# A bidirectional DeltaNet and mLSTM block: another pace for the triangular solve, its inverse stored by quarters, the scan placed later

## The chip, the cores and the metric

The kernel runs on one core of one Trainium2 chip. Its engines are PE (TensorE: matrix products into PSUM), DVE (VectorE), ACT (ScalarE), POOL (GpSimd) and SP (SyncE, which here only issues DMAs). Each runs its own list of instructions in order and waits for the others by semaphores. The metric is device time in microseconds; the kernel before takes 1715.46 us, the median of three runs (1714.88 to 1715.53).

## The reference

One layer on a sequence of 512 tokens of width 2048, all in float32. A normed input is projected to 13,376 columns, which feed two branches: a gated DeltaNet of 8 heads and an mLSTM of 8 heads, each run forward and backward over the sequence; a sigmoid gate mixes them. The change touches the DeltaNet branch:

```python
def gated_delta_chunked(q, k, v, g, beta):          # per direction; chunks of 64 tokens
    gc = jnp.cumsum(g, axis=-1)
    decay = jnp.exp(jnp.where(causal, gc[..., :, None] - gc[..., None, :], -jnp.inf))
    kb = k * beta[..., None]                          # k is l2-normalised over its 128 entries
    lower = jnp.where(strict, jnp.einsum("bhnik,bhnjk->bhnij", kb, k) * decay, 0.0)
    a_mat = lower + jnp.eye(CHUNK, dtype=q.dtype)
    sol = lax.linalg.triangular_solve(a_mat, rhs, left_side=True, lower=True, unit_diagonal=True)
    ...
    def step(state, inp):                             # sequential over the chunks
        v_new = u_c - jnp.einsum("bhlk,bhkv->bhlv", w_c, state)
        state_next = state * jnp.exp(gl_c)[..., None, None] + jnp.einsum("bhlk,bhlv->bhkv", kd_c, v_new)
```

## The kernel before, in words

*The stream.* The weights of all projections are cut into groups of 8 x 128 rows by 128 columns (512 KB). For each group SP loads `wr`, ACT rounds it to `wh`, DVE subtracts to get `wl` (lines 175 and 176), and PE does 24 matmuls of 128 x 512 (line 212). Groups 0 to 47 are the DeltaNet's keys, queries and values (`gk`, `gq`, `gv`), 48 to 63 its output gate `gz`, 64 to 119 the merge gates `mg0` to `mg27`, two groups each, and from 120 on come the mLSTM's inputs. Group n's tiles are called `wr`n, `wh`n and `wl`n. Four `wr` and three pairs of `wh` and `wl` are held.

*The mix.* Everything else is written as one generator, `master()`, and advanced by one `yield` (a tick) after every four matmuls of the stream (`TICK`). So a count of yields is a place in the stream, and the scheduler below that order keeps each engine's list close to it, but moves instructions back where it reckons that their data come later.

*The DeltaNet's part of the mix.* `gdn_pre(h)` forms, per head, the products `pgm`, the sums of squares `pn` and the transposes `px`, and stores what the scan needs in DRAM (`d_head`, `d_lane`). `gdn_solve` then solves all 8 heads x 2 directions x 8 chunks at once: 128 unit triangular matrices of 64 x 64, one per partition of `lx`, in 62 steps of two DVE instructions, `tm` and `lx` (lines 592 and 595). Before the first step the key norm factors are needed: `rk2` from the sums `ssk`, `brk` from it, four transposes to `pb` on PE (line 557), a store to `d_brk` and a load `bsc`. A second form of the factors, `rk` to the power -1/2 on POOL (line 606), gives `cvv` and `csp`, which the scan uses. While the steps run, ACT copies finished columns of `lx` into `l0` and `lt`, which hold the transposed inverse, 16 at a time (`copy_cols`). At the end `lx` and `l0` go to `d_sol`, and `l0` and `lt` to `d_inv` (lines 612 to 622). `gdn_load_b` reads them back per head as `xt` and `xi`.

*The scan.* Heads run in pairs. Each begins with `pw`, 16 small matmuls of `xi` (line 664), then `wx`, a second `pw`, and four chunk pairs of `vps`, `sps`, `kps` and `og`, ending with the transposes `po` (line 745). Three ticks lie between two pieces. After the scan the memory passes to the mLSTM's heads.

Of the kernel before, what the change touches and what calls it, by code (L numbers as in the profile page):

```python
# [9 lines left out]
F32 = mybir.dt.float32  # L10
F32R = mybir.dt.float32r
AF = mybir.ActivationFunctionType
ALU = mybir.AluOpType

P = 128
T = 512
NT = 4
# [3 lines left out]
EPS = 1e-6  # L21
# [8 lines left out]
LOAD_AHEAD = 4  # L30
SPLIT_AHEAD = 2
TICK = 4
SOLVE_RATE = 0.65
N_EARLY = 28


# [4 lines left out]
def hybrid_block(  # L41
# [20 lines left out]
    nc = tc.nc  # L62
# [10 lines left out]
    def pool(name, bufs=1, side="left", space=None):  # L73
        kw = {"space": space} if space is not None else {"side": side}
        if space is None or space == PSUM:
            kw["reuse_waits"] = "tile"
        return tc.tile_pool(name=name, bufs=bufs, **kw)
# [3 lines left out]
    pp = ctx.enter_context(pool("pp", bufs=2, space=PSUM))  # L81
# [4 lines left out]
    d_inv = dram.tile([2, H, 8, 64, 64], F32, name="d_inv")  # L86
# [47 lines left out]
    ones = const.tile([P, 1], F32, name="ones")  # L134
# [99 lines left out]
    egc = const.tile([P, NT, 16], F32, name="egc")  # L234
# [7 lines left out]
    ssk = const.tile([P, NT, H], F32, name="ssk")  # L242
# [215 lines left out]
    def gdn_pre(h):  # L458
        p1 = st["p1"][1]
        if h + 1 < H:  # L460
            dec_load(h + 1)
            qg_load(h + 1)

        dec = st["dec", h]
        dec4 = dec.rearrange("p d (t i) -> p d t i", i=P)
        g4 = gct.rearrange("p t (d h) -> p d t h", d=2)[:, :, :, h:h + 1]
        nc.vector.tensor_tensor(dec4, dec4, g4.broadcast_to([P, 2, NT, P]), op=ALU.subtract)
        for d in range(2):
            nc.gpsimd.affine_select(out=dec4[:, d], in_=dec4[:, d], pattern=[[0, NT], [1 - 2 * d, P]],
                                    compare_op=ALU.is_ge, fill=-1e30, base=0, channel_multiplier=2 * d - 1)  # L470
        for _ in range(3):
            yield
        nc.scalar.activation(dec, dec, AF.Exp)
        while f"gq{h}" not in done:
            yield
        ckq, qg = st["ckq", h], st["qg", h]
        sqt = p1.tile([P, T], F32, tag="sqt", name=f"sqt{h}")
        sqk = p1.tile([P, P], F32, tag="sqk", name=f"sqk{h}")
        for _ in range(4):
            yield  # L480
        nc.scalar.activation(sqt, ckq[:, 1, :], AF.Square)
        for d in range(2):
            nc.gpsimd.tensor_tensor(qg[:, d, :], qg[:, d, :], ckq[:, 1, :], op=ALU.mult)
        while f"gv{h}" not in done:
            yield
        cv = st["cv", h]
        for _ in range(4):
            yield

        pgm = [pp.tile([P, 2, 2, P], F32, tag="mix", name=f"pgm{h}{tt}") for tt in range(2)]  # L490
        for t in range(NT):
            cs = slice(t * P, (t + 1) * P)
            nc.tensor.matmul(pgm[t // 2][:, t % 2], ckq[:, 0, cs], ckq[:, :, cs], start=True, stop=True)
        pn = pp.tile([P, 8], F32, tag="st0", name=f"pn{h}", bufs=1)
        for t in range(NT):
            nc.tensor.matmul(pn[:, t:t + 1], sqt[:, t * P:(t + 1) * P], ones, start=True, stop=True)
        px = [pp.tile([P, NT, P], F32, tag="acc", name=f"px{i}{h}") for i in range(2)]
        for i, src in enumerate((ckq[:, 0, :], cv)):
            for t in range(NT):
                nc.tensor.transpose(px[i][:, t, :], src[:, t * P:(t + 1) * P], ident)  # L500
        la = p1.tile([P, 2, NT, 2, P], F32, tag="la", name=f"la{h}", bufs=2)
        kd = p1.tile([P, 2, NT, P], F32, tag="kd", name=f"kd{h}", bufs=2)
        vt = p1.tile([P, T], F32, tag="vt", name=f"vt{h}", bufs=2)
        nc.scalar.copy(vt, px[1].rearrange("p a b -> p (a b)"))
        for tt in range(2):
            for d in range(2):
                nc.vector.tensor_tensor(la[:, d, tt * 2:tt * 2 + 2], pgm[tt],
                                        dec4[:, d, tt * 2:tt * 2 + 2].unsqueeze(2).broadcast_to([P, 2, 2, P]),
                                        op=ALU.mult)
            yield  # L510
        for t in range(NT):
            nc.scalar.activation(sqk, px[0][:, t, :], AF.Square, accum_out=ssk[:, t, h:h + 1])
        nc.vector.tensor_copy(ssq[:, h, :], pn[:, 0:4])
        for d in range(2):
            nc.vector.tensor_tensor(
                kd[:, d], px[0], ekd[:, :, d * H + h:d * H + h + 1].broadcast_to([P, NT, P]), op=ALU.mult)
        yield
        dh = d_head[h]
        for a in range(2):
            hs_, os_ = half(a), half(1 - a)  # L520
            for d in range(2):
                nc.sync.dma_start(d_lane[d, h, a::2].rearrange("t j i -> j t i"), la[hs_, d, :, 0, hs_])
            nc.sync.dma_start(dh[hs_, HC_Y:HW].rearrange("p (t i) -> p t i", i=64), la[hs_, a, :, 0, os_])
        yield
        nc.sync.dma_start(dh[:, HC_AT:HC_KT].rearrange("p (d t i) -> p d t i", d=2, i=P), la[:, :, :, 1, :])
        nc.sync.dma_start(dh[:, HC_KT:HC_QG], ckq[:, 0, :])
        yield
        nc.sync.dma_start(dh[:, HC_QG:HC_Y], qg.rearrange("p a n -> p (a n)"))
        nc.sync.dma_start(dh[:, HC_V:HC_KD], vt)
        nc.sync.dma_start(dh[:, HC_KD:HC_AT], kd.rearrange("p d t i -> p (d t i)"))  # L530


    cvv = const.tile([P, NT, 2, H], F32, name="cvv")
    csp = const.tile([P, NT, 2, H], F32, name="csp")
    brh = const.tile([P, NT, H], F32, name="brh")

    def gdn_solve():
# [3 lines left out]
        rk = ln.tile([P, NT, H], F32, name="rk")  # L541
        rk2 = ln.tile([P, NT, H], F32, name="rk2")
        brk = ln.tile([P, NT, 2, H], F32, name="brk")
        l0 = ln.tile([P, 64, 64], F32, name="l0")
        lt = ln.tile([P, 64, 64], F32, name="lt")
        nc.sync.dma_start(l0, d_lane.rearrange("d h c j i -> (d h c) j i"))
        nc.vector.tensor_scalar(rk, ssk, EPS, None, op0=ALU.add)
        nc.vector.reciprocal(rk2, rk)
        beta4 = beta.rearrange("p t (d h) -> p t d h", d=2)
        bc = lambda v: v.unsqueeze(2).broadcast_to([P, NT, 2, H])  # L550
        nc.vector.tensor_scalar(rk2, rk2, -1.0, None, op0=ALU.mult)
# [22 lines left out]
        yield  # L574


        rev = l0[64:128, ::-1, ::-1]
        tr0 = l0[0:64].rearrange("p m j -> p j m")
        tr1 = lt[64:128].rearrange("p m j -> p j m")[:, ::-1, ::-1]
# [2 lines left out]
        def copy_cols(n, q):  # L582
            to, of = copies[n]
            cs = slice(q * 16, q * 16 + 16)
            nc.scalar.copy(to[:, :, cs], of[:, :, cs])

        cost = 0.0
        for c in range(1, 63):
            n = 63 - c
            tm = ln.tile([P, 1024], F32, tag="tm", name=f"tm{c}", bufs=1)  # L590
            tv = tm[:, 0:c * n].rearrange("p (j i) -> p j i", i=n)
            nc.vector.tensor_tensor(  # L592
                tv, lx[:, 0:c, c:c + 1].broadcast_to([P, c, n]),
                lx[:, c:c + 1, c + 1:64].broadcast_to([P, c, n]), op=ALU.mult)
            nc.vector.tensor_tensor(lx[:, 0:c, c + 1:64], lx[:, 0:c, c + 1:64], tv, op=ALU.add)  # L595
            cost += 0.13 + 0.0021 * c * n
            while cost > 0:
                yield
                cost -= SOLVE_RATE
            if 20 <= c < 60 and c % 5 == 0:  # L600
                next(st["la", 0])
            if c > 16 and c % 16 in (1, 3, 5):
                copy_cols(c % 16 // 2, c // 16 - 1)
            if c == 30:

                nc.gpsimd.tensor_tensor(rk, rk, mhalf.rearrange("p (t h) -> p t h", h=H), op=ALU.pow)
            if c == 60:
                nc.vector.tensor_tensor(cvv, beta4, bc(rk), op=ALU.mult)
                nc.vector.tensor_scalar(rk, rk, -1.0, None, op0=ALU.mult)
                nc.vector.tensor_tensor(csp, egc.rearrange("p t (d h) -> p t d h", d=2), bc(rk), op=ALU.mult)  # L610
        lanes = lambda v: v.rearrange("h c j i -> (h c) j i")
        nc.sync.dma_start(lanes(d_sol[0]), lx[0:64])
        nc.vector.tensor_copy(rev[:, :, 48:64], lx[64:128, :, 48:64])
        yield
        copy_cols(0, 3)
        nc.scalar.dma_start(lanes(d_inv[0]), l0[0:64])
        yield
        yield
        nc.sync.dma_start(lanes(d_sol[1]), l0[64:128])
        yield  # L620
        copy_cols(2, 3)
        nc.scalar.dma_start(lanes(d_inv[1]), lt[64:128])
        for _ in range(10):
            yield
        close_pool("ln")
# [301 lines left out]
    def master():  # L927
        yield from setup()
        for h in range(H):
            yield from gdn_pre(h)  # L930
# [3 lines left out]
        gdn_load_b(0)  # L934
        gdn_load_b(1)
        st["la"] = itertools.chain(gdn_load_a(2), gdn_load_a(3))
        for _ in range(6):
            yield
        yield from rolling([together([gdn_head(h), gdn_head(h + 1)]) for h in range(0, H, 2)], 13, 3)
        close_pool("p2")  # L940
# [358 lines left out]
```

## Time and profile before

| | |
|---|---|
| median of three runs | 1715.46 us |
| profiled execution | 1713.81 us |
| its span, first to last instruction | 1712.1 us |
| PE busy | 1670.8 us (98%) |
| DVE busy | 866.6 us (51%) |
| ACT busy | 618.5 us (36%) |
| POOL busy | 82.4 us (5%) |
| mean granted TensorE clock | 0.994 |

The share of an engine is an average over stages, so it is read by stretch. The page's row of PE in 40 slices has full slices but for the first, slice 13 (514 to 556 us) and the last; in slice 13 the row of the granted clock has its only value below 9. The chain that ended last goes through PE for 89% of the span, DVE for 6% and DMAs for 2%.

### The profile page before, as it was taken

The page shows a single profiled execution, that of the slowest core. Times are in us where ns is not written, and L with a number is a line of the kernel's source. Part 1 is how long each engine was busy: PE and PEld are TensorE (multiplying, and loading weights), DVE is VectorE, ACT ScalarE, POOL GpSimd, SP SyncE. Part 2 cuts the span into 40 slices and gives each one's busy share as a digit, 9 for nine tenths or more (in the row PEclk, how much of TensorE's full clock was granted, in tenths as well). Part 3 has the DMA queues.
Part 4 walks back from the last instruction along what each step waited for, and adds up shares of the span by engine and source line. Part 5 has one row for each costly group of instructions (what it writes and reads, how often), then busy time and mean ns, then how long its engine had stood idle before and what let it go on. Part 6 is the DMA issues. An engine that isn't in the chain of part 4 may idle for free.

```text
span 1712.1 us, 20938 instructions
## 1 busy us (share of the span) xinstructions
PE 1670.8 (98%) x8250; PEld 1403.1 (82%) x8250; DVE 866.6 (51%) x1266; ACT 618.5 (36%) x917; POOL 82.4 (5%) x117
## 2 busy tenths in 40 slices
PE   6999999999996999999999999999999999999998
PEld 6788888878884888888888888888888888888886
DVE  6865556569992433332345445454544444443342
ACT  6654444323432222343343344244333422222231
POOL 1100110010000000010000000000000000000000
PEclk9999999999998999999999999999999999999999
DMA  7577776594447875354443344344334644454222
GB/s 189 151 214 195 178 182 180 147 300 126 113 116 180 273 216 168 103 154 125 108 111 106 104 111 111 99 111 116 82 98 132 203 146 148 148 175 169 98 99 99
DMA packets 333724, 251.93 MB, mean 147 GB/s; under 512 B 38872, under 2 KB 294233, under 8 KB 332473
## 3 DMA queue, kind: packets, MB, share of 16 engines
q1 hardware_dynamic: 327952, 238.39, 48.8%
q10 hardware_dynamic: 5673, 12.19, 2.2%
q8 instruction: 65, 1.06, 0.3%
q14 instruction: 34, 0.28, 0.0%
HBM read 207.32 MB, written 43.16 MB: 146 GB/s over the span
## 4 chain that ended last, share of the span: by engine, by line
PE 89%; DVE 6%; issue 2%; DMA 2%; ACT 1%; POOL 0%; POOLq 0%; DVEq 0%; ACTq 0%; SPq 0%
PE pj_m L212 25%; PE pj_mg L212 15%; PE pj_br L212 10%; PE wo L1052 10%; PE pj_gq L212 5%; PE pj_gv L212 5%; PE pj_gk L212 4%; PE pj_gz L212 3%; DVE lx L595 2%; DVE tm L592 2%; PE og L683 1%; DVE wl L176 1%; DMA d_inv<-lt 1%; PE vps L706 1%; PE ph L885 1%
## 5 line engine op out<-in xcount | busy, mean ns | idle before, releaser
L176 DVE TENSOR_TENSOR wl<-wr,wh 128x1024 fp32r<-128x1024 f32 x270 | 332.1, 1231 | 474.7 <-ACT wh L175 132.7
L175 ACT CAST wh<-wr 128x1024 fp32r<-128x1024 f32 x270 | 284.0, 1052 | 710.4 <-PE pj_m L212 209.2
L212 PE MATMUL pj_m<-nth,wh 128*128 128x512 f32 x640 | 250.7, 392 | 0.0
L212 PE MATMUL pj_m<-ntl,wh 128*128 128x512 f32 x640 | 249.5, 390 | 0.0
L212 PE MATMUL pj_mg<-nth,wh 128*128 128x512 f32 x512 | 202.0, 395 | 0.0
L212 PE MATMUL pj_mg<-ntl,wh 128*128 128x512 f32 x512 | 200.6, 392 | 0.0
L212 PE MATMUL pj_m<-nth,wl 128*128 128x512 f32 x640 | 160.3, 391 | 0.0
L212 PEld LDWEIGHTS pj_m<-nth,wh 128*128 128x128 f32 x640 | 120.2, 188 | 24.6
L212 PEld LDWEIGHTS pj_m<-ntl,wh 128*128 128x128 f32 x640 | 120.3, 188 | 24.2
L212 PEld LDWEIGHTS pj_m<-nth,wl 128*128 128x128 f32 x640 | 119.6, 188 | 24.6
L212 PE MATMUL pj_mg<-nth,wl 128*128 128x512 f32 x512 | 130.7, 398 | 0.0
L212 PEld LDWEIGHTS pj_mg<-nth,wh 128*128 128x128 f32 x512 | 96.4, 188 | 19.6
L212 PEld LDWEIGHTS pj_mg<-ntl,wh 128*128 128x128 f32 x512 | 96.4, 188 | 19.2
L212 PEld LDWEIGHTS pj_mg<-nth,wl 128*128 128x128 f32 x512 | 95.8, 190 | 19.3
L1052 PE MATMUL wo<-wh,mh 128*128 128x512 f32 x256 | 100.1, 391 | 0.0
L1052 PE MATMUL wo<-wh,ml 128*128 128x512 f32 x256 | 99.8, 390 | 0.0
L212 PE MATMUL pj_br<-yl,wh 128*128 128x512 f32 x256 | 99.7, 390 | 0.0
L212 PE MATMUL pj_br<-yh,wh 128*128 128x512 f32 x256 | 99.7, 389 | 0.0
L1052 PE MATMUL wo<-wl,mh 128*128 128x512 f32 x256 | 72.9, 390 | 0.0
L1017 DVE TENSOR_TENSOR mgr<-pj_br,mgr 128x512 f32<-128x512 f32 x32 | 22.1, 692 | 86.5 <-PE pj_br L212 86.5
L212 PE MATMUL pj_br<-yh,wl 128*128 128x512 f32 x256 | 63.2, 389 | 0.0
L1052 PEld LDWEIGHTS wo<-wl,mh 128*128 128x128 f32 x256 | 48.1, 188 | 10.5 <-DVE wl L176 0.2
(320 smaller groups left out, 2515.2 us busy)
## 6 DMA issues: line engine op xcount, KB each, us to landing
wr<-in_w_in_dram SPq DMA_DIRECT2D x206, 512.0 KB, 4.0
wr<-in_w_out_dram SPq DMA_DIRECT2D x32, 512.0 KB, 4.1
hr<-d_head SPq DMA_DIRECT2D x16, 768.0 KB, 7.7
d_gate<-gt ACTq DMA_DIRECT2D x32, 256.0 KB, 4.2
e<-d_row SPq DMA_DIRECT2D x8, 1024.0 KB
mgr<-d_gate SPq DMA_DIRECT2D x32, 256.0 KB, 3.5
wr<-in_w_branch_gdn_dram SPq DMA_DIRECT2D x16, 512.0 KB, 4.8
wr<-in_w_branch_mlstm_dram SPq DMA_DIRECT2D x16, 512.0 KB
```

The lines of the kernel that those rows point to most:

```text
L175: nc.scalar.copy(hi[:, 0:m], self.raw[:, 0:m])
L176: nc.vector.tensor_tensor(lo[:, 0:m], self.raw[:, 0:m], hi[:, 0:m].bitcast(F32), op=ALU.subtract)
L212: nc.tensor.matmul(ps[0:m, :], l, r, start=(first and n == 0), stop=(last and n == len(jobs) - 1))
L592: nc.vector.tensor_tensor(tv, lx[:, 0:c, c:c + 1].broadcast_to([P, c, n]), lx[:, c:c + 1, c + 1:64].broadcast_to([P, c, n]), op=ALU.mult)
L595: nc.vector.tensor_tensor(lx[:, 0:c, c + 1:64], lx[:, 0:c, c + 1:64], tv, op=ALU.add)
L683: nc.tensor.matmul(po[:, t], l, r, start=not opened, stop=last)
L706: nc.tensor.matmul(vps[:, d], xt[:, d, t], rhs[d], start=True, stop=True)
L885: nc.tensor.matmul(ph[:, j - q0, :], e4[:, d, 0, t, :], vv[:, t, :], start=(n == 0), stop=True)
L1017: nc.vector.tensor_tensor(g_, ps, g_, op=ALU.mult)
L1052: nc.tensor.matmul(ps, l[:, kt, ts_], r, start=(kt == 0 and l is mh and r is hv), stop=(kt == NK - 1 and r is lv))
```

## The change

The solve's steps are spread by a lower rate, which is what one tick takes off a step's reckoned cost. `pn` is written behind the `px` transposes. `rk2` gets its own addition, and `rk`, its power, `cvv` and `csp` are placed at steps 30 and 50 of the solve, behind that step's `tm`. Each quarter of the inverse is stored right behind its copy, on ACT's queue, and the two stores of the whole are gone. The scan begins 18 ticks after the solve in place of 6.

```diff
-SOLVE_RATE = 0.65
+SOLVE_RATE = 0.56
...
-        pn = pp.tile([P, 8], F32, tag="st0", name=f"pn{h}", bufs=1)
-        for t in range(NT):
-            nc.tensor.matmul(pn[:, t:t + 1], sqt[:, t * P:(t + 1) * P], ones, start=True, stop=True)
         px = [pp.tile([P, NT, P], F32, tag="acc", name=f"px{i}{h}") for i in range(2)]
         for i, src in enumerate((ckq[:, 0, :], cv)):
             for t in range(NT):
                 nc.tensor.transpose(px[i][:, t, :], src[:, t * P:(t + 1) * P], ident)
+        pn = pp.tile([P, 8], F32, tag="st0", name=f"pn{h}", bufs=1)
+        ...
-        nc.vector.tensor_scalar(rk, ssk, EPS, None, op0=ALU.add)
-        nc.vector.reciprocal(rk2, rk)
+        nc.vector.tensor_scalar(rk2, ssk, EPS, None, op0=ALU.add)
+        nc.vector.reciprocal(rk2, rk2)
...
             nc.scalar.copy(to[:, :, cs], of[:, :, cs])
+            if n != 1:
+                src, r0 = (l0[0:64], q * 16) if n == 0 else (lt[64:128], 48 - q * 16)
+                nc.scalar.dma_start(lanes(d_inv[n // 2])[:, r0:r0 + 16], src[:, r0:r0 + 16])
...
             if c == 30:
+                with tc.issue_after(step.ins if hasattr(step, "ins") else step):
+                    nc.vector.tensor_scalar(rk, ssk, EPS, None, op0=ALU.add)
                 nc.gpsimd.tensor_tensor(rk, rk, mhalf.rearrange("p (t h) -> p t h", h=H), op=ALU.pow)
-            if c == 60:
-                ...
+            if c == 50:
+                with tc.issue_after(step.ins if hasattr(step, "ins") else step):
+                    nc.vector.tensor_tensor(cvv, beta4, bc(rk), op=ALU.mult)
+                    nc.vector.tensor_scalar(rk, rk, -1.0, None, op0=ALU.mult)
+                    nc.vector.tensor_tensor(csp, egc.rearrange("p t (d h) -> p t d h", d=2), bc(rk), op=ALU.mult)
...
         copy_cols(0, 3)
-        nc.scalar.dma_start(lanes(d_inv[0]), l0[0:64])
...
         copy_cols(2, 3)
-        nc.scalar.dma_start(lanes(d_inv[1]), lt[64:128])
...
-        for _ in range(6):
+        for _ in range(18):
             yield
```

What stands in DVE's list between the gates `ga0` and the split `wl53`, ahead of the solve, before and then in the change:

```order
L547 TENSOR_SCALAR rk_2850<-ssk_138 128x32
L548 RECIPROCAL rk2_2851<-rk_2850 128x32
L551 TENSOR_SCALAR rk2_2851<-rk2_2851 128x32
L608 TENSOR_TENSOR cvv_140<-tgs_129,rk_2850 128x64
L552 TENSOR_TENSOR brk_2852<-tgs_129,rk2_2851 128x64
L609 TENSOR_SCALAR rk_2850<-rk_2850 128x32
L572 COPY brh_142<-brk_2852 64x32
L573 COPY brh_142<-brk_2852 64x32
```

```order
L547 TENSOR_SCALAR rk2_2851<-ssk_138 128x32
L548 RECIPROCAL rk2_2851<-rk2_2851 128x32
L551 TENSOR_SCALAR rk2_2851<-rk2_2851 128x32
L552 TENSOR_TENSOR brk_2852<-tgs_129,rk2_2851 128x64
L572 COPY brh_142<-brk_2852 64x32
L573 COPY brh_142<-brk_2852 64x32
```

`cvv`, which takes POOL's result, no longer stands ahead of `brk`; it and `rk`'s sign are placed at step 50.

ACT's list at the end of the solve, from the last copy into `l0`, before and then in the change:

```order
L585 COPY l0_2853<-lx_2909 64x64x16
L585 COPY lt_2854<-lx_2909 64x64x16
L616 DMA d_inv_68<-l0_2853 64x4096
L622 DMA d_inv_68<-lt_2854 64x4096
L983 ACTIVATE gt7_4167<-pj_mg7_4013,vec_118 128x512
L175 CAST wh83_4217<-wr83_4062 128x1024
L984 DMA d_gate_76<-gt7_4167 128x512
L983 ACTIVATE gt8_4278<-pj_mg8_4176,vec_118 128x512
```

```order
L586 COPY l0_2853<-lx_2909 64x64x16
L987 ACTIVATE gt7_4072<-pj_mg7_3988,vec_118 128x512
L589 DMA d_inv_68<-l0_2853 64x1024
L988 DMA d_gate_76<-gt7_4072 128x512
L586 COPY lt_2854<-lx_2909 64x64x16
L175 CAST wh83_4111<-wr83_4026 128x1024
L589 DMA d_inv_68<-lt_2854 64x1024
L175 CAST wh84_4168<-wr84_4075 128x1024
L987 ACTIVATE gt8_4163<-pj_mg8_4081,vec_118 128x512
L988 DMA d_gate_76<-gt8_4163 128x512
```

The two stores of 64 x 4096 are stores of 64 x 1024, and the store of the gate `gt7` stands between them.

PE's list where the scan's first `pw` stands, before and then in the change:

```order
L664 MATMUL pw0_4084<-xi0_4025,hr0_3194 64x64
L212 MATMUL pj_mg9_4287<-ntl_128,wh82_4172 128x512
L212 MATMUL pj_mg9_4287<-nth_127,wl82_4173 128x512 x8
L212 MATMUL pj_mg9_4287<-nth_127,wh83_4217 128x512
L664 MATMUL pw0_4084<-xi0_4025,hr0_3194 64x64 x7
```

```order
L212 MATMUL pj_mg10_4236<-nth_127,wl84_4169 128x512 x8
L668 MATMUL pw0_4273<-xi0_4146,hr0_3230 64x64 x8
L668 MATMUL pw1_4296<-xi1_4156,hr1_3713 64x64 x8
L212 MATMUL pj_mg10_4236<-nth_127,wh85_4199 128x512
```

Between the two places lie nine more matmuls of group 82 and the 48 of groups 83 and 84; `pw` of head 1 now follows at once. On SP the load of `wr87` now stands ahead of the first `xt`, and that of `wr88` behind the last `xi` of head 1; before, both stood behind all of `hr2` and `hr3`.

## Rows read from the trace of the kernel before

**Rows 1.** Waits of PE, whole run: engine, line, releaser, total us, times, longest.

```profile
PE pw L664 <- DMA xi<-d_inv: 16.2, 1, 16.2
...
PE pb L557 <- DVE rk L609: 2.6, 1, 2.6
...
PE pn L496 <- ACT sqt L481: 1.2, 1, 1.2
```

**Rows 2.** Stretches: busy us of each engine, granted clock, DMA share, GB/s.

```profile
348.00:351.00 3.00, 0.40 (x4) 0.27 (x4) 0.74 (x5) 0.00 (x0) 2.18 (x1) 1.00 1.14 454
402.00:516.00 114.00, 114.00 (x505) 94.45 (x504) 108.17 (x114) 41.96 (x38) 0.00 (x0) 1.00 0.44 120
543.00:544.00 1.00, 1.00 (x4) 0.50 (x2) 0.01 (x1) 0.00 (x0) 0.00 (x0) 0.50 0.52 118
544.00:545.00 1.00, 1.00 (x16) 0.69 (x16) 1.00 (x1) 0.00 (x0) 0.00 (x0) 0.84 0.35 80
540.00:740.00 200.00, 200.00 (x1359) 173.80 (x1359) 77.51 (x159) 56.56 (x130) 9.73 (x14) 0.99 0.59 177
```

**Rows 3.** Timeline of PE: start, us, engine, line, operation, count, idle before.

```profile
517.78 1.98 PE L212 MATMUL pj_mg<-nth,wl 128*128 128x512 f32 x8
...
522.76 0.39 PE L212 MATMUL pj_mg<-nth,wh 128*128 128x512 f32 x1
539.31 0.44 PE L664 MATMUL pw<-xi,hr 64*64 64x64 f32 x2 [16.16 <-DMA xi<-d_inv]
```

**Rows 4.** Timeline of ACT at the solve's end (ACTq: its DMA issues).

```profile
512.50 2.07 ACT L585 COPY l<-lx 64x1024 f32<-64x1024 f32 x1 [4.35 <-DVE lx L595]
...
514.60 0.51 ACTq L616 DMA_DIRECT2D d_inv<-l  x1
516.66 1.06 ACTq L622 DMA_DIRECT2D d_inv<-lt  x1
```

**Rows 5.** Waits of SP, the DMA queue, 500 to 560 us.

```profile
SPq L643 <- DMA d_sol<-l: 8.8, 1, 8.8
...
SPq L644 <- DMA d_inv<-lt: 3.8, 1, 3.8
...
SPq L643 <- DMA d_inv<-l: 3.3, 1, 3.3
```

**Rows 6.** Timeline of SP's DMA issues.

```profile
514.47 1.89 SPq L166 DMA_DIRECT2D wr<-in_w_in_dram  x1
...
535.71 0.57 SPq L644 DMA_DIRECT2D xi<-d_inv  x1
...
538.25 0.57 SPq L644 DMA_DIRECT2D xi<-d_inv  x1
...
542.16 0.61 SPq L644 DMA_DIRECT2D xi<-d_inv  x1
```

**Rows 7.** The tile xi: its loads, from issue to landing.

```profile
DMA to landing us min/median/max: 2.4/2.4/2.4
```

**Rows 8.** DMA queues, 514 to 522, then 522 to 526: packets, MB, share.

```profile
q1 hardware_dynamic: 115, 1.62, 94.1%
...
q10 hardware_dynamic: 45, 0.74, 71.2%
```

**Rows 9.** Timeline of DVE before the solve.

```profile
344.31 0.35 DVE L548 RECIPROCAL rk<-rk 128x32 f32<-128x32 f32 x1
...
350.22 0.23 DVE L608 TENSOR_TENSOR cvv<-tgs,rk 128x64 f32<-128x64 f32 x1 [5.34 <-POOL rk L606]
350.36 0.22 DVE L552 TENSOR_TENSOR brk<-tgs,rk 128x64 f32<-128x64 f32 x1
```

**Rows 10.** Timeline of ACT, head 0.

```profile
80.49 0.61 ACT L481 ACTIVATE sqt<-ckq 128x512 f32<-128x512 f32 x1
```

**Rows 11.** Chain that ended last, the scan's end and the mLSTM's first projection.

```profile
751.53 0.87 PE po L745 x8
...
822.23 34.46 PE pj_m L212 x152
```

More of the change, by code (lines that the diff above doesn't have):

```diff
@@ L500, in gdn_pre @@
                 nc.tensor.transpose(px[i][:, t, :], src[:, t * P:(t + 1) * P], ident)
+        pn = pp.tile([P, 8], F32, tag="st0", name=f"pn{h}", bufs=1)
+        for t in range(NT):
+            nc.tensor.matmul(pn[:, t:t + 1], sqt[:, t * P:(t + 1) * P], ones, start=True, stop=True)
         la = p1.tile([P, 2, NT, 2, P], F32, tag="la", name=f"la{h}", bufs=2)
@@ L574, in gdn_solve @@
         yield
+        lanes = lambda v: v.rearrange("h c j i -> (h c) j i")
         rev = l0[64:128, ::-1, ::-1]
@@ L591, in gdn_solve @@
             tv = tm[:, 0:c * n].rearrange("p (j i) -> p j i", i=n)
-            nc.vector.tensor_tensor(
+            step = nc.vector.tensor_tensor(
                 tv, lx[:, 0:c, c:c + 1].broadcast_to([P, c, n]),
@@ L604, in gdn_solve @@
             if c == 30:
+                with tc.issue_after(step.ins if hasattr(step, "ins") else step):
+                    nc.vector.tensor_scalar(rk, ssk, EPS, None, op0=ALU.add)
                 nc.gpsimd.tensor_tensor(rk, rk, mhalf.rearrange("p (t h) -> p t h", h=H), op=ALU.pow)
-            if c == 60:
[L608 to L611, printed above, removed]
+            if c == 50:
[3 more added lines that the diff above has]
+                    nc.vector.tensor_tensor(csp, egc.rearrange("p t (d h) -> p t d h", d=2), bc(rk), op=ALU.mult)
         nc.sync.dma_start(lanes(d_sol[0]), lx[0:64])
```

## The prediction

> **What bounds the kernel now.** I read the busy line of the page first: PE works 1670.8 of 1712.1 us, so only the 41.3 us in which it stands still, and any time at a lowered clock, can be given back. The list of who waited for whom, for PE alone, came next [rows 1]: one wait of 16.2 us at the first `pw` matmul (line 664), which opens the scan and waits for `xi`, the inverse read back from `d_inv`; 2.6 us at `pb` (line 557) for the key norm factors; 1.2 us at the `pn` sums (line 496). The rest lies in the start and at the end, which the change leaves alone. Third, the table by stretches [rows 2]: between 402 and 516 us DVE works 108.17 of 114 us, so the solve runs there without a gap and its end cannot be pulled forward by another order. From 540 to 740 us, the scan, PE has no idle time at all.
>
> The stall costs more than its length. PE's timeline shows it between 522.99 and 539.31 us [rows 3], and the granted clock is 0.50 in 543 to 544 and 0.84 in 544 to 545 [rows 2]: 0.84 of the second at the two levels 0.5 and 1.0 puts the return to the 2.4 GHz level at 544.3. So from 539.3 to 544.3 PE worked at the 1.2 GHz level, and 5.0 us of work hold 2.5 us of loss. Round the shorter stall at `pb` the clock stayed at 1.00 [rows 2].
>
> Who sets the 539.31? The solve ends at 512.50, where ACT, released by DVE's `lx`, starts the last copies; the two 1 MB writes of `d_inv` leave ACT's queue at 514.60 and 516.66 [rows 4]. SP, which issues the loads, has sent off `wr86` by 516.4 [rows 6] and then waits 8.8 us for the second `d_sol` write, to 525.2, 3.3 for `d_inv<-l` and 3.8 for `d_inv<-lt` [rows 5]. `xi` of head 0 goes out at 535.71 and 538.25, the last of head 1 at 542.16 [rows 6]; each lands 2.4 us later [rows 7].
>
> **The change, part by part.** *The inverse by quarters.* Two writes of 1 MB become eight of 256 KB, six of them issued during the solve. After the solve 0.5 MB is left in place of 2 MB. The queue rows show when that is moved [rows 8]: from 514 to 522 us the data packets are queue 1's (SP: the `d_sol` writes) and none are queue 10's (ACT), though `d_inv<-l` was issued at 514.60; queue 10 moves 0.74 MB from 522 to 526. I therefore reckon the ACT queue's data behind the 2 MB of `d_sol`, from 522.5 on (estimate: queue 10's 0.74 MB at 71.2% of that stretch's 4 us took nearly all of it). The second `d_inv` write landed some 7.1 us after the first (528.6, where SP's 3.3 us wait ends, to 535.7): 7.1 us per MB.
>
> The order on ACT at the end of the solve puts a gate write between the two last quarters, so `lt`'s quarter is the third 256 KB of queue 10: 0.75 x 7.1 = 5.3 us. Four small DVE instructions (`rk`, `cvv`, `rk`, `csp`, about 0.2 us each by the rows of their like [rows 9]) move from before the solve into the stretch where DVE has no gap: the solve ends 0.8 us later against PE. So 522.5 + 0.8 + 5.3 = 528.6, and 1.5 us until the writer's end is seen (an estimate: SP is released from `d_sol` at 525.2, some 2 us after queue 10 took over the engines): `xi` of head 0 may go out at 530.1. The six other writes cost ACT 0.5 to 1.1 us of issue each, as the two of before [rows 4]; ACT is busy 41.96 of the 114 us [rows 2], so that is hidden.
>
> *A rule weighed here.* The Trainium skill, page "DMA: Bandwidth & Descriptors", section "Queues, rings and completion order", says that each DMA engine takes turns between the queues that have work for it. Rows 8 speak against equal turns here, since ACT's queue got nothing for eight microseconds. By the rule the quarters would be through before `d_sol`, and the wait below would be gone.
>
> *The scan placed later, and the solve's rate.* The rate goes from 0.65 to 0.56. The solve's 95.6 units of cost then take 171 ticks of four stream matmuls in place of 147, and 18 ticks follow in place of 6. On DVE the order of solve steps and weight splits stays as it was but for single places, so I count the rate itself at nothing, between -1 and +1 us: DVE is full there either way. What moves is PE's order. `pw` of head 0 stood after the fifteenth matmul of group 82; now it stands after the last of group 84, which is 9 + 24 + 24 = 57 matmuls later. From 517.78 to 522.76 there are 22 matmuls [rows 3], 0.2264 us each, so PE gets there 12.9 us later, at 535.9 on the old trace's time. (All that moves earlier, below, moves PE and the solve alike.)
>
> Against that: the second load of `xi` for head 0 goes out 2.54 us after the first and lands 2.4 us later [rows 6, 7], 530.1 + 4.9 = 535.0, in time. Head 1's last goes out 6.45 us after the first: 530.1 + 6.45 + 2.4 = 538.95, while PE, after head 0's 16 small matmuls (some 0.55 us), wants it at 536.45. A wait of 2.5 us stays. Bounds: none, if ACT's queue is served beside `d_sol`; and 8.1 us, if the quarters help nothing and `xi` goes out at 535.71 as now (544.55 - 536.45).
>
> Queued behind on SP are the weight loads: `wr87` now goes ahead of `xt`, `wr88` behind `xi1`. If SP is held until 537, `wr88` lands by about 543, 512 KB taking 4.0 us by the page's list of DMA issues. Groups 85 to 87 lie in between on PE, at 5.4 us each without and about 9 us with the scan's pieces, so group 88 starts after 560. Hidden, with some 17 us to spare.
>
> *Key norm factors.* In the old order the pow on POOL fed `cvv`, which stood in DVE's queue ahead of `brk`: DVE idles 5.34 us and `brk` ends at 350.6 [rows 9]. Now `brk` follows the reciprocal: 344.31 + 0.35 + 0.2 + 0.2 puts its end near 345.2, which is 5.4 us earlier, twice what PE waited [rows 1]. The 2.6 us go. The solve does not start earlier against PE by this: `bsc`, which releases it, stands on SP behind the store of `ga1`, which PE's stream paces. The pow, now at step 30, has 20 steps of over 2 us before step 50 needs it; 5.4 us are covered.
>
> *`pn` behind the transposes.* For head 0 PE waits 1.2 us for `sqt`, which ends at 81.10 [rows 10]. Four `px` transposes go ahead of it there, 0.11 us each, 0.45 us of the wait filled. For the other heads nothing waits.
>
> *Later work.* The scan's end moves 140 stream matmuls, 31.7 us. Its last `po` was at 751.53, the first `pj_m` at 822.23 [rows 11], so some 39 us of room are left before the mLSTM heads need the buffers. I count 0, with up to +1 us for an odd wait in the scan.
>
> **The sum.** Idle at `pw` 16.16 - 2.5 = 13.7; clock 2.5 (a wait of 2.5 us should cost none, as at `pb`); `pb` 2.6; `pn` 0.45: 19.2 us. The profiled execution took 1713.81 us, its span 1712.1; that gives a span of 1692.9 and an execution of 1694.6. The median of the runs is 1.65 above the profiled execution, so **1696.2 us**. What is late next is PE itself, 1668 us of work in a span of 1693.
>
> **The rivals.**
> *A: nothing waits at `pw`.* The quarters share the engines with `d_sol`, or 4 KB rows pass faster. For it: a gate write of 256 KB on queue 10 lands in 4.2 us by the page's list of issues, beside weight loads. Against: rows 8. The 2.5 us go too: 1693.7. The Trainium skill's rule of turns, from the page named above, would come out here as well.
> *B: the wait stays long.* The loads of `xi` wait for the late gate writes or for `wr86` and `wr87`, whose 1 MB of short packets shares the queue. Wait of 5 to 8 us, and the clock falls again for part of it: 16.16 - 7 = 9.2, clock 1, `pb` and `pn` 3.05, together 13.2: 1702.
> *C: slower.* The weight loads that now lie among `xt`, `xi` and `hr` come late. `hr2` and `hr3` are 4.5 MB, `wr88` to `wr95` 4 MB, beside a stream that takes a group about every 9 us there. It decides once a load lands later than the 17 us to spare allow; six groups 4.5 us late each would cost 27 us, more than is saved: 1696.2 + 27 = 1723. Against: in the old order all of `hr2` and `hr3` stood ahead of `wr87`, and PE never waited from 540 to 740 [rows 2].
> *D: it doesn't do what it says.* The rate alone does not move DVE's order, as above; if the quarters also change nothing, the later place of `pw` alone still hides 12.9 of the 16.2 us, which is B's upper end.
>
> **Chances.** Forecast (wait of 0.7 to 5 us, 1694.3 to 1698.6) 0.50; A 0.27; B with D 0.17; C 0.03; something unseen that eats all 0.03. About 0.2% (3.4 us) is what a measurement of this kernel tells from no change. Faster 0.94, same 0.03, slower 0.03. The range of 8 in 10 takes in A, with half a microsecond for the terms counted at nothing, and B: 1692.5 to 1702.5.
>
> **What would show it.** Right: `pb` gone from PE's waits; `pw` at 0 to 5 us, waiting for `xi1`; a granted clock of 1.00 after it; PE's idle time near 25 us in all; scan and mLSTM stretches as before. Wrong: queue 10 moving data before `d_sol` ends (A), `pw` waiting over 5 us (B), PE waits at `wh` or `wl` of groups 88 to 95 (C).

## The result and the profile after

The changed kernel takes 1694.2 us (median of four runs, 1693.28 to 1694.8) against 1715.49 of the kernel before on the same chip: a ratio of 0.9875 [0.9858, 0.9892], 21.3 us faster. The forecast was 1696.2. A later series of the same kernel gave 1693.09. The profiled execution took 1693.68 us with a span of 1691.9; PE is busy for 1669.0 us of it, so it stands still for 22.9 us where it stood still for 41.3, and works 1.8 us less.

The waits of PE over the whole run, after (engine, line, releaser, total us, times, longest; code moved down by four lines, so `pw` is line 668):

```profile
PE pv L1168 <- DMA v<-in_gdn_norm_w_dram: 8.3, 1, 8.3
PE xtp L1150 <- DVE xdg L1139: 2.2, 1, 2.2
PE xtp L1152 <- DVE x L1143: 1.7, 1, 1.7
PE px L497 <- ACT cv L445: 1.0, 2, 0.6
PE pn L500 <- ACT sqt L481: 0.5, 1, 0.5
PE pw L668 <- DMA xi<-d_inv: 0.3, 1, 0.3
```

Beside [rows 1]: `pw` has gone from 16.2 to 0.3 and `pb` is gone. `pn` shows 0.5 in place of 1.2, and `px`, whose transposes now go first, waits 1.0 us for ACT's `cv`; these two change from kernel to kernel under one order (see e5). The rest is the start of the kernel. PE's timeline where [rows 3] had the stall:

```profile
532.69 1.98 PE L212 MATMUL pj_mg<-nth,wl 128*128 128x512 f32 x8
534.59 0.79 PE L668 MATMUL pw<-xi,hr 64*64 64x64 f32 x18
535.72 0.67 PE L668 MATMUL pw<-xi,hr 64*64 64x64 f32 x14 [0.33 <-DMA xi<-d_inv]
```

Head 0's sixteen and two of head 1's go through at once, and only head 1's second half waits. The stretches of [rows 2] (busy us of PE, PEld, DVE, ACT, POOL, granted clock, DMA share, GB/s):

```profile
402.00:516.00 114.00, 114.00 (x505) 94.39 (x504) 106.84 (x118) 42.51 (x39) 6.36 (x1) 1.00 0.50 134
543.00:544.00 1.00, 1.00 (x6) 0.83 (x5) 0.50 (x1) 0.56 (x1) 0.00 (x0) 1.00 0.43 96
544.00:545.00 1.00, 1.00 (x6) 0.85 (x5) 0.72 (x1) 0.13 (x1) 0.00 (x0) 1.00 0.45 104
540.00:740.00 200.00, 200.00 (x1322) 174.60 (x1319) 75.18 (x154) 58.54 (x130) 8.49 (x14) 1.00 0.60 183
```

The granted clock (1.00 is its 2.4 GHz level) stays at 1.00, and PE still has no gap in the scan. On ACT the solve ends at 509.62, where the last copy into `l0` starts; the answer to [rows 4]:

```profile
509.62 2.07 ACT L586 COPY l<-lx 64x1024 f32<-64x1024 f32 x1 [2.87 <-DVE lx L599]
...
511.71 0.45 ACTq L589 DMA_DIRECT2D d_inv<-l  x1
512.21 2.57 ACTq L988 DMA_DIRECT2D d_gate<-gt  x1
514.82 2.04 ACT L586 COPY lt<-lx 64x1024 f32<-64x1024 f32 x1 [2.67 <-issue]
...
516.88 0.45 ACTq L589 DMA_DIRECT2D d_inv<-lt  x1
```

SP's issues, as in [rows 6] (`wr87`'s halves, then `xt` and `xi` of heads 0 and 1):

```profile
511.59 7.99 SPq L166 DMA_DIRECT2D wr<-in_w_in_dram  x2
524.64 1.54 SPq L647 DMA_DIRECT2D xt<-d_sol  x2
527.33 0.57 SPq L648 DMA_DIRECT2D xi<-d_inv  x1
...
529.27 0.61 SPq L648 DMA_DIRECT2D xi<-d_inv  x1
...
533.32 0.61 SPq L648 DMA_DIRECT2D xi<-d_inv  x1
```

The first `xi` goes out 17.71 us behind the solve's end (527.33 - 509.62); before, it was 23.21 (535.71 - 512.50). Head 1's last lands after 2.4 us, 533.32 + 2.4 = 535.72, which is the moment PE goes on. What SP waited for there (500 to 560 us; [rows 5] of before):

```profile
SPq L647 <- DMA d_inv<-l: 4.9, 1, 4.9
...
SPq L648 <- DMA d_inv<-lt: 1.1, 1, 1.1
```

The queues of [rows 8], by two microseconds (512 to 514, 518 to 520, 522 to 524; packets, MB, share of the 16 engines):

```profile
q1 hardware_dynamic: 30, 0.49, 120.1%
...
q1 hardware_dynamic: 25, 0.41, 139.4%
q10 hardware_dynamic: 1, 0.00, 0.5%
...
q10 hardware_dynamic: 141, 0.29, 67.8%
```

As before, ACT's queue (10) moves nothing from 511.71, when its quarter was issued, until about 520, while SP's queue (1) writes `d_sol`.

### The profile page after: what moved, and what is told of

Read it like the earlier page. It is cut to its first block, busy times and chain, and to the rows that moved or that the text cites. A ratio compares the mean times of both kernels' runs of the same rounds, so it can differ in the third digit from the quotient of the medians.

```text
span 1691.9 us, 20945 instructions
## 1 busy us (share of the span) xinstructions
PE 1669.0 (99%) x8250; PEld 1401.7 (83%) x8250; DVE 864.9 (51%) x1267; ACT 619.6 (37%) x917; POOL 83.7 (5%) x117
## 4 chain that ended last, share of the span: by engine, by line
PE 85%; DVE 8%; DMA 3%; issue 3%; ACT 1%; SPq 0%; ACTq 0%; POOL 0%; DVEq 0%; POOLq 0%
PE pj_m L212 26%; PE pj_mg L212 14%; PE pj_br L212 10%; PE wo L1056 10%; PE pj_gq L212 5%; PE pj_gv L212 4%; PE pj_gk L212 4%; PE pj_gz L212 3%; DVE lx L599 2%; DVE tm L596 2%; DVE wl L176 2%; PE og L687 1%; DMA wr<-in_w_in_dram 1%; PE vps L710 1%; PE ph L889 1%
## 5 line engine op out<-in xcount | busy, mean ns | idle before, releaser
L212 PEld LDWEIGHTS pj_m<-nth,wl 128*128 128x128 f32 x640 | 119.6, 188 | 24.6
L212 PE MATMUL pj_mg<-nth,wl 128*128 128x512 f32 x512 | 126.7, 389 | 0.0
L212 PEld LDWEIGHTS pj_mg<-ntl,wh 128*128 128x128 f32 x512 | 96.3, 188 | 18.4
```

Source lines behind the costliest of these rows:

```text
L212: nc.tensor.matmul(ps[0:m, :], l, r, start=(first and n == 0), stop=(last and n == len(jobs) - 1))
```

## Experiments

All kernels compute the whole result. "Place" is where the first `pw` stands in PE's list, in stream matmuls behind its place before; "solve" is from the start of the first `lx` product to the start of the last copy into `l0`; "xi" is the issue of head 0's first `xi` behind that. The last three are from the profiled execution.

| kernel | median us | place | wait at `pw` us | solve us | xi us |
|---|---|---|---|---|---|
| before | 1715.5 | 0 | 16.2 | 151.94 | 23.21 |
| after | 1694.2 | +57 | 0.3 | 150.36 | 17.71 |
| e1, scan's place alone | 1715.39 | 0 | 16.2 | 151.89 | 23.26 |
| e2, quarters alone | 1704.25 | +23 | 4.2 | 150.33 | 16.32 |
| e3, key factors alone | 1711.32 | 0 | 16.2 | 151.76 | 23.27 |
| e4, after without the rate | 1700.66 | +23 | 4.1 | 150.34 | 16.16 |
| e5, after without `pn`'s move | 1693.32 | +57 | 0.6 | 150.45 | 18.01 |
| e6, after without quarters | 1701.84 | +57 | 5.6 | 150.81 | 24.04 |
| e7, after without the scan's place | 1700.61 | +23 | 4.8 | 150.28 | 17.88 |
| e8, `d_sol` behind `d_inv` | 1694.85 | +57 | 1.2 | 150.44 | 19.72 |
| e10, rate alone | 1709.83 | +35 | 10.5 | 150.78 | 24.56 |
| r_after | 1693.09 | +57 | 0.5 | 150.49 | 17.89 |
| e9, two edits more | 1691.0 | +73 | 0 | 150.50 | 17.78 |
| e11, e8 with `xi` first | 1692.04 | +57 | 0 | 150.48 | 18.17 |

e1 to e4 ran on one chip (before 1714.87), e5 to e8 on a second (1715.41), the last four on a third (1715.49).

**The scan's place alone (e1_later).**

```diff
-        for _ in range(6):
+        for _ in range(18):
```

> The kernel before with the scan 18 ticks behind the solve in place of 6, nothing else. In PE's order the first pw stays behind the same 2078th matmul of the stream as before. Theory (pw's wait is set by its place in PE's list and by the landing of xi, and here neither moves): 16 us of wait at pw, 1715 us, within 1 us of before. Rival (the 18 ticks by themselves put 12.9 us of stream ahead of pw, as the prediction had it): a wait of 3 to 4 us, 1702 us.

1715.39 us, ratio 1.0001 [0.9992, 1.001]. PE's list has `pw` in the same place as before: twelve ticks more in `master()` moved nothing, and the stall is that of before.

```profile
538.78 0.44 PE L664 MATMUL pw<-xi,hr 64*64 64x64 f32 x2 [16.20 <-DMA xi<-d_inv]
```

So the ticks by themselves don't give the 57 matmuls; with the rate changed too they do matter (e7). The scheduler moves instructions back where it reckons that their data come later, and if that place lay behind the one that the ticks ask for, they would move nothing; its reckoning shows in no run.

**The quarters alone (e2_quarters).**

```diff
             nc.scalar.copy(to[:, :, cs], of[:, :, cs])
+            if n != 1:
+                src, r0 = ...
+                nc.scalar.dma_start(lanes(d_inv[n // 2])[:, r0:r0 + 16], src[:, r0:r0 + 16])
...
-        nc.scalar.dma_start(lanes(d_inv[0]), l0[0:64])
...
-        nc.scalar.dma_start(lanes(d_inv[1]), lt[64:128])
```

> The kernel before with the inverse stored by quarters, nothing else. PE's order has the first pw 23 matmuls (5.2 us) later than before, at 2101. Theory: PE is there near 528.2 us, xi of head 0 lands near 532.6 (20.1 us behind the solve's end, as in the changed kernel), so some 4 to 5 us of wait stay, and the clock falls for little of it: 1702 us. Rival (the quarters alone do all of it): no wait at pw, 1697 us. Other rival (they do nothing without the rest): 1715 us.

1704.25 us, 0.9936 [0.9921, 0.995]: 10.6 us, half the gain, from this edit by itself. `xi` goes out 6.9 us sooner behind the solve's end, `pw` moves 23 places back, and the solve is 1.6 us shorter. The time is 2 us above the expected 1702, because the wait that stays still costs clock. PE's timeline, the first two `pw` of head 0:

```profile
534.04 0.30 PE L665 MATMUL pw<-xi,hr 64*64 64x64 f32 x2 [4.22 <-DMA xi<-d_inv]
...
538.34 0.68 PE L665 MATMUL pw<-xi,hr 64*64 64x64 f32 x14
```

Ten stream matmuls lie in between, and the second group of `pw` starts 4.30 us after the first; at 0.2264 us each the ten would take 2.3.

**The key norm factors alone (e3_tie).** `rk2` has its own addition, and `rk`, `cvv` and `csp` stand at steps 30 and 50, as in the change.

> The kernel before with the key norm factors tied into the solve (rk2 by itself, rk, cvv and csp at steps 30 and 50), nothing else. Theory: the 2.6 us of PE's wait at pb go and the solve moves forward with PE, so the wait at pw stays 16 us: 1712.9 us. Rival (the solve's end does not move, so the pb time comes back at pw, which then waits 18.8 us): 1715.5 us.

1711.32 us, 0.9979 [0.9969, 0.9989]. In its profile `pb` is gone and `pw` waits as before. The gain of 3.6 us has an interval from 1.9 to 5.3 and so agrees with the 2.6 us of the wait. (The profiled execution was the slowest of e3's nine, 1714.88 us, so the gain is read from the median alone.) `brk` no longer stands behind POOL; DVE's timeline of the changed kernel, beside [rows 9]:

```profile
345.64 0.35 DVE L548 RECIPROCAL rk<-rk 128x32 f32<-128x32 f32 x1
...
346.25 0.23 DVE L552 TENSOR_TENSOR brk<-tgs,rk 128x64 f32<-128x64 f32 x1
```

**The change without the rate (e4_rate065), and without the scan's place (e7_scan6).**

```diff
-SOLVE_RATE = 0.56
+SOLVE_RATE = 0.65
```

```diff
-        for _ in range(18):
+        for _ in range(6):
```

> The changed kernel with the solve's rate back at 0.65. PE's order then has the first pw at 2101 in place of 2135, and ACT's list has the weight cast wh78 behind the third quarter's copies of l0 and lt. Theory: the rate is not free of effect; PE comes to pw 7.7 us earlier, and DVE's solve ends some 1.5 us later because a weight split waits behind the copies again: 5 to 6 us of wait at pw, 1699.5 us. Rival (the rate is worth nothing, as the prediction counted it): 1694.2 us.

> The changed kernel with the scan 6 ticks behind the solve again; rate 0.56 kept. PE's order has pw at 2101. Theory: PE is there 7.7 us earlier, near 526.9, xi of head 0 lands near 529.7 to 530 and head 1's last near 535.7: 4 us of wait in all, 1698 us. Rival (the rate alone gives the place): 1694.2 us.

1700.66 us, 0.9912 [0.9897, 0.9927], and 1700.61, 0.9919 [0.9903, 0.9936]. Against the kernel before on their chips they gain 14.2 and 14.8 us, where the change gains 21.3. So either of the two taken back alone puts `pw` at +23 and costs some 6.5 to 7.1 us, more than expected. They are not two terms that add: the full place needs both. The expectation had the solve end 1.5 us later with the old rate, but its length stayed at 150.34: the weight cast does stand behind the copies again, but DVE's split stands later in its list too, and does not wait. Here too the wait brings the clock down; e4 in 530 to 534 and 534 to 538 us, with its wait ending at 531.30:

```profile
530.00:534.00 4.00, 2.70 (x8) 2.13 (x9) 0.00 (x0) 1.04 (x1) 0.00 (x0) 0.50 0.44 97
534.00:538.00 4.00, 4.00 (x25) 2.87 (x24) 1.56 (x2) 0.69 (x1) 0.00 (x0) 0.70 0.45 101
```

**The rate alone (e10_rate).** The kernel before with 0.56 for 0.65.

> The kernel before with the solve's rate at 0.56 and nothing else changed. Theory (the rate moves the place of the scan, which the ticks alone did not): pw stands 35 stream matmuls later, 7.9 us, so its wait is 16.2 - 7.9 = 8.3 us, or 6.7 where the solve also ends up to 1.6 us sooner; the clock's 2.5 us stay, pb's 2.6 stay: 1706 to 1707.5. Rival (the prediction: the rate counts nothing, between -1 and +1): 1714.5 to 1716.5.

1709.83 us (1707.45 to 1711.88), 0.9966 [0.9956, 0.9977]: 5.7 us faster, which the prediction's 0 ± 1 excludes; the expectation of 1706 to 1707.5 missed too. PE comes to `pw` 19.66 us behind the solve's end (10.65 before), 9.0 later: 7.9 by the place and 1.2 by the shorter solve. Yet the wait is 10.5, and not 8.3 or less (the row finds no releaser for it):

```profile
542.96 0.45 PE L664 MATMUL pw<-xi,hr 64*64 64x64 f32 x2 [10.47 <-issue]
```

The way of the inverse has become 3.3 us longer: `pw` starts 30.1 us behind the solve's end, 26.8 before. ACT's order changed with the rate: a gate store stands between the two halves, and its issue holds ACT.

```profile
514.92 0.51 ACTq L616 DMA_DIRECT2D d_inv<-l  x1
515.47 2.55 ACTq L984 DMA_DIRECT2D d_gate<-gt  x1
518.07 2.04 ACT L585 COPY lt<-lx 64x1024 f32<-64x1024 f32 x1 [2.72 <-issue]
...
520.14 0.45 ACTq L622 DMA_DIRECT2D d_inv<-lt  x1
```

`d_inv<-lt` leaves 7.3 us behind the solve's end (4.2 before), the first `xi` 24.56 us behind it (23.21), and `xi` takes 3.8 us to land where it took 2.4.

**The change with whole stores (e6_whole).**

```diff
-            if n != 1:
-                ...
...
+        nc.scalar.dma_start(lanes(d_inv[0]), l0[0:64])
...
+        nc.scalar.dma_start(lanes(d_inv[1]), lt[64:128])
```

> The changed kernel with the inverse stored whole, in two writes of 1 MB after the solve, as before. pw stays at 2135. Theory: xi of head 0 goes out 23.2 us behind the solve's end, as in the kernel before, and not 17.7: waits of about 3 us at head 0's pw and 3 us at head 1's, 1700.5 us. Rival (the later place of pw hides all of it): 1694.2 us.

1701.84 us, 0.9925 [0.991, 0.9939], some 8 us more than with quarters. `xi` is back at 24.04 us behind the solve's end. With 4 MB to write after the solve (`d_sol` and the whole inverse) it leaves at 23.2 to 24.6, with 2.5 MB (and `d_sol` on SP's queue) at 16.2 to 18.0: the earlier issue goes with the fewer bytes left behind the solve. The time missed the expected 1700.5 by 1.3 us.

**The change with `pn` ahead again (e5_pnback).**

```diff
+        pn = pp.tile([P, 8], F32, tag="st0", name=f"pn{h}", bufs=1)
+        ...
         px = [pp.tile([P, NT, P], F32, tag="acc", name=f"px{i}{h}") for i in range(2)]
```

> The changed kernel with pn back ahead of the px transposes. Theory (pn's matmuls were what PE did while ACT finished cv; moved behind, they leave two waits at px): the waits of px on cv go, pn of head 0 waits 1.2 us again, and the pgm of head 7 comes about 1.1 us earlier: 1693.1 us. Rival (the prediction's term, 0.45 us gained by the move): 1694.7 us.

1693.32 us, 0.9875 [0.986, 0.989]: no difference that can be told from the changed kernel. The `px` waits are gone and `pn` waits 1.1, as expected, but that can't be put down to the move. The two waits together are 0.5 to 1.6 us in the seven kernels with `pn` ahead (0.5 in e1, whose edit lies elsewhere) and 0.6 to 1.6 in the seven with it behind, of which e4 and e7 have 1.2 at `pn` and no wait at `px`.

**`d_sol` on ACT's queue, behind the inverse (e8_solbehind).**

```diff
-        nc.sync.dma_start(lanes(d_sol[0]), lx[0:64])
...
-        nc.sync.dma_start(lanes(d_sol[1]), l0[64:128])
...
         copy_cols(2, 3)
+        nc.scalar.dma_start(lanes(d_sol[0]), lx[0:64])
+        nc.scalar.dma_start(lanes(d_sol[1]), l0[64:128])
```

> The changed kernel with the two d_sol writes issued on ACT's queue behind the last quarter of d_inv, in place of on SP's queue ahead of it. Theory (a write's data move only when the writes issued before it are through, on whichever queue): the last quarters of d_inv move by 513 us, at once after their issue, and d_sol's 2 MB behind them until 526 or later; SP's loads of xt, which stand ahead of xi, then go out 3 to 5 us later than now, and pw waits 3 us or so: 1697 us. Rival (ACT's queue is slow by itself, or the queues take turns): queue 10 moves nothing of d_inv before 518 us.

1694.85 us, 0.9883 [0.9868, 0.9898]. The queues in 514 to 516 us, 2.6 us after the quarter's issue at 511.43:

```profile
q10 hardware_dynamic: 187, 0.51, 63.2%
q1 hardware_dynamic: 601, 0.30, 50.1%
```

With `d_sol` off SP's queue, ACT's queue moves its data some six microseconds sooner, in the same stretch as SP's weight loads. (ACT's order came out with the first `d_sol` store, 512.59, ahead of the last quarter of the inverse, 514.63.) The time lies below the expected 1697. Yet the first `xi` leaves later (19.72): SP now waits for the second `d_sol` store ahead of the first `xt`.

```profile
SPq L647 <- DMA d_sol<-l: 11.4, 1, 11.4
```

**The same with `xi` loaded ahead of `xt` (e11_xifirst).**

```diff
         for a in range(2):
+            nc.sync.dma_start(xi[half(a)], d_inv[a, h, a::2].rearrange("t j i -> j t i"))
+        for a in range(2):
             for d in range(2):
                 nc.sync.dma_start(xt[half(a), d, :, half(a)], ...)
-            nc.sync.dma_start(xi[half(a)], ...)
```

> The changed kernel with the d_sol writes on ACT's queue behind the last quarter of the inverse (as in e8_solbehind), and with the loads of xi ahead of those of xt. Theory (a write of ACT's queue that was issued behind SP's 2 MB of d_sol gets the engines only when that is through; with d_sol behind it, the quarters move at once, as queue 10's 0.51 MB in 514 to 516 of e8 show): head 0's first xi goes out 8 to 12 us behind the solve's end in place of 17.7, pw waits 0; the time stays within 0.5 us of the changed kernel, since only some 0.3 us were left there. Rival (the writer's end is seen late for another reason, such as the gate store's long issue on ACT or the wr loads on SP): the first xi 16 us or more behind the solve's end.

1692.04 us, 0.9865 [0.985, 0.988], as the changed kernel. The first `xi` left at 18.17 us and not at 8 to 12, so that expectation fell, though `xi` reads nothing of `d_sol`. POOL, which fills `xt` with zeros and reads nothing at all, is released by the same store, within 0.3 us of `xi`'s issue at 526.94:

```profile
527.20 2.83 POOL L643 MEMSET xt<- 64x256 f32 x8 [84.89 <-DMA d_sol<-l]
```

By the code, `xt` and `xi` lie in a pool that is opened when the solve's is closed, so they can take `l0`'s memory only when the last store has read it. That fits both rows, and the changed kernel too, where SP's `xt`, which reads `d_sol`, waited 4.9 us for `d_inv<-l`; a kernel with separate memory was not tried. The run is no clean test of the queues, either: as in e8, ACT's order came out as `d_inv<-l`, `d_sol<-lx`, `d_inv<-lt`, `d_sol<-l`, so the second quarter had 1 MB ahead of it after all.

**The changed kernel again (r_after), and with two edits (e9_pn_scan22).** `pn` ahead of `px`, and 22 ticks in place of 18.

> The changed kernel once more, beside the three below on one chip, so that differences of half a microsecond can be told. Theory (place and solve's end decide the wait at pw): 1693.3 to 1694.8 as before, pw wait of 0.0 to 0.7 us, the solve (first lx product to last copies) 150.2 to 150.6 us, head 0's first xi 17.5 to 18.0 us behind its end. Rival (the 1.6 us shorter solve was an accident of the one profiled execution): solve near 152 us again and a pw wait near 2.5 us, which the prediction reckoned with.

> The changed kernel with pn written ahead of the px transposes as before, and the scan 22 ticks after the solve in place of 18: pw stands 16 stream matmuls (3.6 us) later. Theory: pw waits 0 (0.3 to 0.6 us now), px's two waits of 1.0 us go, pn's 0.5 becomes 1.1: 0.3 to 1.0 us faster than the changed kernel, about 1693.3. Rival (the room behind the scan is used up, the mLSTM's first products wait for memory): a new wait of over 1 us between 740 and 830 us and a time of 1695 or more.

1693.09 us (1692.1 to 1694.86) and 1691.0 (1690.73 to 1691.28), 0.9871 [0.9858, 0.9885] and 0.9858 [0.9845, 0.9872] of before. The solve of r_after is again 150.5 us, so its shortening was no accident. e9 has no wait at `pw`, none at `px`, and one of 0.8 at `pn`. It has the lowest median here, and its runs don't overlap those of r_after beside it (1692.1 at the least), but the two intervals do: that it is faster is likely and not shown. The 2.1 us between them are 0.12%, and the waits account for only some 0.3 us of them (`pw` 0.5 and `px` 0.3 less, `pn` 0.5 more). Where the rest comes from is open.

## Why the prediction held, and where not

The mechanism was right: the stall at `pw` with its clock, and `pb`, were the gain. By its steps:

- **Idle at `pw`, 13.7 forecast:** 15.8 measured (16.16 - 0.33). This is the term of the sum that was mis-sized, and the step that failed is "the solve runs there without a gap and its end cannot be pulled forward by another order". DVE's 108.17 of 114 us [rows 2] left 5.8 us, and 1.9 of it were waits for ACT. The forecast had the solve end 0.8 us later against PE; it is 1.6 us shorter. The 0.8 us counted for the four small instructions don't show either: e3 has them in the solve, and it takes 151.76 us there against 151.94. Where the solve became shorter shows at the split that follows the third quarter's copies. The timeline of all engines, before:

```profile
488.84 2.10 ACT L585 COPY lt<-lx 64x1024 f32<-64x1024 f32 x1
...
490.96 1.05 ACT L175 CAST wh<-wr 128x1024 fp32r<-128x1024 f32 x1
...
492.05 1.23 DVE L176 TENSOR_TENSOR wl<-wr,wh 128x1024 fp32r<-128x1024 f32 x1 [1.54 <-ACT wh L175]
```

  and after:

```profile
487.16 1.05 ACT L175 CAST wh<-wr 128x1024 fp32r<-128x1024 f32 x1
...
488.25 1.22 DVE L176 TENSOR_TENSOR wl<-wr,wh 128x1024 fp32r<-128x1024 f32 x1 [0.49 <-ACT wh L175]
...
488.82 2.07 ACT L586 COPY lt<-lx 64x1024 f32<-64x1024 f32 x1
```

  `wh` now stands ahead of the copy into `lt`, so `wl`, and the solve steps behind it, wait 1.05 us less; a second wait of 0.37 at 445.56 is gone too: 1.4 of the 1.6 us. e2 and e10, with one edit each, have shorter solves as well (150.33 and 150.78), e1 and e3, which keep the wait, do not. In e2 it is gone by another way: `wh` still stands behind the copy, but `wl` stands later in DVE's list (496.21) and waits for nothing. PE reaches `pw` 24.97 us behind the solve's end, where the forecast had 22.6: the 2.4 us more that emptied the wait.
- **The way of the inverse:** forecast, the first `xi` leaves at 530.1 for a solve that ends at 513.3, 16.8 us; measured 17.71, and 17.89 in r_after. ACT's data lay behind `d_sol` as reckoned. Rival A's time came about, but not by its mechanism.
- **The place of `pw`:** 57 matmuls, as read from the order. What moves it was put wrong: "I count the rate itself at nothing". The rate alone is worth 5.7 us (e10), taking it back costs some 6.5 (e4), and the ticks alone nothing (e1). For the sum it made no difference, since the place was read for the whole change. For rival D it did: both of its parts have an effect, and its price of 1702 was met only with one of the three edits taken back (1700.6 to 1701.8).
- **The clock, 2.5:** PE is busy 1.8 us less, and works at 1.00 after `pw`. That "a wait of 2.5 us should cost none, as at `pb`" was not put to the test, and is not safe: see the last section.
- **`pb`, 2.6:** gone, and e3 agrees.
- **`pn`, 0.45:** the wait fell by 0.7, but the transposes ahead of it wait 1.0 for `cv`, which the step did not look at. In r_after the two are 0.3 and 0.3, and other kernels scatter as widely (e5). The term is not measurable.
- **Rival C and later work:** no wait at `wh` or `wl` of groups 88 to 95, none from 540 to 740 us. From the last `po` to the first `pj_m` there are 39.0 us (762.65 to 801.62), the room that the forecast left.
- **Total:** 15.8 + 2.6 - 0.3 = 18.1 of idle time, beside the 18.4 that PE's idle time fell, and 1.8 of clock: 20.2 us of span, 19.2 forecast. Of the 2.0 us between 1696.2 and 1694.2 the other 1.1 is that the median of before lies 1.65 us above its profiled execution, and that of after 0.52.

*The rule of turns.* After and e10 show what [rows 8] showed: a write on ACT's queue, issued behind SP's 2 MB, moves nothing for seven or eight microseconds. Packet size is not the reason in e10, where the inverse moves in 16 KB packets, as `d_sol` does (16 packets, 0.26 MB in 522 to 524). e8 shows the two queues working in one stretch when SP's holds short weight packets. The Trainium skill, page "DMA: Bandwidth & Descriptors", section "Queues, rings and completion order", has each engine take turns between queues, and lets it drain a whole packet of one queue, typically some 9 to 17 descriptors, before it switches. The prediction read this as short turns ("the quarters would be through before `d_sol`"), and such turns e8 shows and the others do not. But the page's packet need not be the profile's. If each 16 KB packet of the rows is one descriptor, `d_sol`'s 2 MB are 128 of them, 8 for each of 16 engines: by the page's figure, as an estimate, they could all fall into one turn, and then no run here contradicts the page. How long a turn is no run shows, and what decides between the two pictures was not isolated.

## What to carry to other kernels

Where one engine's data are late for another, look at three distances from one common event, here the end of the solve: when the reader comes, when the data leave, and what the event itself waits for; an engine that is 95% busy can still be waiting in the chain that counts. Moving stores ahead of such an event paid here with the bytes that were left behind it. And attribute a place in an order to an edit only by reading the order of each edit alone: here the rate alone gave 35 matmuls, the stores alone 23 and the ticks alone none, while all edits together gave 57, and still 57 without the stores (e6).

## What the runs showed of the hardware

*Two short waits can cost clock where a longer one costs none.* e8 waits 0.57 and 0.60 us at `pw`, and then has stretches (PE's busy us, granted clock) of

```profile
537.00:538.00 1.00, 0.69 (x15) 1.00 0.60 108
538.00:539.00 1.00, 1.00 (x3) 0.64 1.12 337
539.00:540.00 1.00, 1.00 (x4) 0.50 1.18 318
540.00:541.00 1.00, 1.00 (x4) 0.50 1.22 288
541.00:542.00 1.00, 1.00 (x10) 0.65 1.38 204
```

Its eight stream matmuls from 538.26 to 541.76 took 3.5 us in place of 1.8. At `pb` of before, 2.6 us of waiting left the clock at 1.00 [rows 2], and so did single waits at the same `pw` matmuls: 0.33 us after the change, and 0.64 in e5. So neither the length of a wait nor the small matmuls explain it alone. e8 has two waits, 1.2 us apart; whether that is what counts was not tested.

*Issuing a store can hold ACT for 2.6 us.* The gate store between the last quarters took 2.57 us to issue where it took 0.33 earlier in the solve, and ACT's next copy waited 2.67 us for it. In e8 it took 0.60, and the second store of `d_sol` took the 2.61.
